# A neighbourhood-attention and Fourier layer: first matmuls on ones, keys in equal pieces, a later split of the u tiles, and another order of the last tile's VectorE work

## The chip, the cores and the metric

The kernel runs on one core of one Trainium2 chip. The metric is the time of one execution in microseconds (us) on the device. It is the median of several runs; the run with a profile is one more execution and has its own time.

## What is computed

The reference is one encoder layer on 256 prompt tokens and, with the same weights, on 2048 sample tokens of width 1024:

```python
h = rms_norm(x, g_pre)
q, k, v, z_a, u_f, z_f = split(h @ w_in)          # six parts, 512 columns each
y_a = neighbourhood_attention(q, k, v, rpb)       # 8 heads of 64, window of 8 x 16 on a grid 64 wide
y_f = fourier_mix(u_f, w_f, b_f)                  # real part of fft2 over tokens and 64-column groups, then @ w_f + b_f
mixed = concat([rms_norm(y_a, g_na) * silu(z_a), rms_norm(y_f, g_f) * silu(z_f)])
x + rms_norm(mixed @ w_out, g_post)
```

All inputs and outputs are float32. A query of the attention sees a slab of 8 grid rows by 32 columns; what lies outside of its own window is masked before the softmax.

## The kernel before, in words

**Products.** A float32 operand is split in a high part, rounded to the type `fp32r`, and a low part, the rest. Every large product is three matmuls on these parts (`mm3`, L163 to L166): high by high (L164), high by low (L165), low by high (L166). The cast to the high part is ScalarE's and the subtraction that gives the low part is VectorE's: `x_split` (L283, L284) for the input tiles `xh` and `xl`, `split_w` (L253, L254) for the weights `wc`, L550 and L551 for the later weights `wa`.

**Order.** The order of TensorE's instructions is that of the code from beginning to end. For the other engines it is that of the code in some stretches (the one with the u tiles and the one of the last output tiles among them) and left to a scheduler elsewhere. Each engine runs its own list in order and waits for what its next instruction needs. SyncE (SP) issues the loads and stores, in the same way.

**Stages.** First the v and u projections of the first input tiles, whose operands must first be loaded and split; the row scales of the norm are spread over partitions by matmuls with a 128x128 tile of ones (`onesq`, filled on GpSimd at L226, used at L309). Then the remaining projections for the sample tokens, in 16 steps `i`, each of seven products `j` of 12 matmuls. Into the steps 9 to 14 the u tiles are woven. Then the Fourier mixing, the attention together with the output product of earlier tiles, and at the end the 18 output tiles of 128 tokens.

**u tiles.** There are 16 of them. A tile is loaded (`u_load`, L364 to L368), split (`u_split`: cast to the high part on ScalarE at L371, low part on VectorE at L372) and multiplied with the first Fourier matrix (`u_stage1`: three matmuls into `pz`, a copy, a store to `ZD`). L915 says when: the tile whose load stands ahead of product x is split three products later and multiplied five products later. In the same products VectorE and ScalarE split the next weights (`wa`, L550 and L551), VectorE does the sums after a product (`u` at L931, `f` at L854), and the bias tables of the attention are prepared: at one product of a step the VectorE subtraction of `t_mask` (L585, tile `mt`), then its three GpSimd additions (L589).

**Attention.** Four head pairs by nine groups of 256 queries: the prompt, and row blocks R0 to R3 in two halves each. A group has two column blocks `b` with `n` keys each: 160 and 160 for the prompt; 264 and 352 (or 352 and 264) in R0; 360 and 480 in R1 and R2; 288 and 384 in R3. The keys are cut in pieces of 128 and a rest (`prep_v`, L1126 to L1131): the pieces of `v` are loaded with the key on the partition, by one DMA for the full pieces and one for the rest. `transp` (L1454) turns the probabilities `w` into `pt` piece by piece on TensorE (L1460) and copies them out of PSUM, one head on ScalarE (L1462) and one on VectorE; `pv` (L1468) multiplies piece by piece (L1476), the key being the contracted dimension, so that a matmul uses as many rows of the array as its piece has keys.

**End.** The last output tile (`last_tile`, L1666) has its second half in two products of 384 and 128 columns (L1673). After each, `evac` (L1627 on VectorE, L1630 on ScalarE) scales it, adds, and sums squares. `residual(b, n)` (L1661) finishes the two halves of the tile before it.

Of the kernel before, what the change touches and what calls it, by code (L numbers as in the profile page):

```python
# [10 lines left out]
F32 = mybir.dt.float32  # L11
# [157 lines left out]
def build(tc, A, O):  # L169
    nc = tc.nc  # L170
# [42 lines left out]
    ps = es.enter_context(tc.tile_pool(name="ps", bufs=3, space=PSUM))  # L213
# [7 lines left out]
    onesq = hp.tile([128, 128], F32, name="onesq")  # L221
    csm = hp.tile([128, 80], F32, name="csm")
    rmask = hp.tile([128, 48], F32, name="rmask")
    nc.gpsimd.memset(onesq, 1.0)

    def gt(shape, dtype, name):  # L226
        return gp.tile(shape, dtype, tag="g", name=name)
# [401 lines left out]
    for kp in range(4):  # L629
        ks = slice(2 * kp, 2 * kp + 2)  # L630
        v = part(RV[kp // 2], kp)
# [107 lines left out]
    for b in range(16):  # L739
# [11 lines left out]
        if b < 8:  # L751
            x, y = divmod(b, 2)
# [7 lines left out]
        p = mmt(512)[:, :TP]  # L760
# [3 lines left out]
        o = st.tile([128, 256], F32, tag="f", name="f", bufs=3)  # L764
        if kind % 2:
            i, d = p, o
        else:
            i = p.rearrange("p (b r c) -> p b r c", b=2, c=32)
            d = o.rearrange("p (r b c) -> p b r c", b=2, c=32)
# [46 lines left out]
    for i in range(16):  # L816
# [15 lines left out]
        o = [st.tile([128, 1024], F32, tag="f", name="f", bufs=3) for x in range(2)]  # L832
# [32 lines left out]
        for j in range(7):  # L865
            if i in (0, 8):
                if j in (0, 3):
                    w_load(i + 1 + j // 3)
                if i == 0 and j == 0:
                    a_split(0, 6)  # L870
                if i == 0 and j == 1:
                    row_scales(10, 8)
                if i == 0 and j == 2:
                    diag_group(1)
                if i == 0 and j == 4:
                    spread_group(1)
                if j == 2:
                    w_sums(i + 1)
                for x in {3: (0, 1), 4: (2, 3), 5: (4, 5), 6: (6,)}.get(j, ()):
                    a_split(i + 1, x)  # L880
            elif i not in (7, 15):
                if j == 0:
                    w_sums(i + 1)
                a_split(i + 1, j)
                if j == 3 and i < 14 and i != 6:
                    w_load(i + 2)
            elif i == 7:
                if j in (3, 4):
                    op_load(j - 3)
                if j in (5, 6):  # L890
                    op_split(j - 5)
                if j == 5:
                    wo_load(0)
            if sg == 0:
                x, y = divmod(7 * (pr - 1) + j, 14)
                if x in (0, 1):
                    if y == 0:
                        n_load(x)
                    elif 3 <= y < 7:
                        n_scale(x, *divmod(y - 3, 2))  # L900
                    elif 7 <= y < 12:
                        n_diff(x, y - 7)
                if pr == 6 and j in (2, 5):
                    (b_split if j > 2 else b_get)(0)
                if pr == 7 and j:
                    b_get(j)
                    if j > 2:
                        b_split(j - 2)
            if i == 2 and j == 0:
                for t, n in ((gmix, "gmix"), (bfs, "bf"), (dnyq, "dnyq"), (rmask, "rmask"), (csm, "csmask")):  # L910
                    nc.sync.dma_start(t, A[n])
                nc.sync.dma_start(cm, A["cmask"].rearrange("p (b x) -> p b x", b=2))
            if i == 5 or 8 <= i < 15:
                t_step(max(0, i - 7), j)
            for f, d in ((u_load, 0), (u_split, 3), (u_stage1, 5)):  # L915
                x = 7 * pr + j - 7 - d
                if sg and 0 <= x < 36 and x % 7 in (0, 2, 4):
                    f(x // 7 * 3 + x % 7 // 2)
            if i == 15 and j in (1, 3, 4, 5):
                if j == 1:  # L920
                    d2 = [load_d(0), load_d(1)]
                else:
                    zgs.append(load_z(j - 3))
            if 9 <= i < 15 and j == 2:
                v_copy(i - 9)
            p = mmt(512)
            aw = aop[i, j]
            bh, bl = bnew[sg, j]
            for k in range(4):
                mm3(nc, p, aw[:, 0, k], aw[:, 1, k], bh[:, k], bl[:, k], k == 0, k == 3)  # L930
            add = lambda o, u: nc.vector.tensor_tensor(out=e_(o), in0=uu[u], in1=p, op=ALU.add)  # L931
            if j == 0:
                nc.scalar.copy(e_("u0"), p)
            elif j == 1:
                comb(0, 0, "u0", p)
            elif j == 2:
                add("u2", "u0")
            elif j == 3:
                add("u4", "u2")
            elif j == 4:  # L940
                comb(1, 1, "u4", p)
                add("u3", "u2")
            elif j == 5:
                comb(1, 0, "u3", p, ALU.subtract)
                store(1)
            else:
                comb(0, 1, "u4", p)
                store(0)
# [165 lines left out]
    def prep_v(g):  # L1114
        cs = slice(g["pr"] * 128, g["pr"] * 128 + 128)
        g["v"] = jl.tile([128, 7, 128], F32, tag="v", name="v", bufs=VB)
        g["ch"], j = [], 0
        for b, (c0, w) in enumerate(g["t"]):
            n = g["nr"] * w
            if g["R"] is None:  # L1120
                src = vP[b]
            else:
                src = vD[2 * g["hc"] + b][K0[g["R"]]:K0[g["R"]] + g["nr"]]
            src = src.rearrange("r c e -> (r c) e")
            f = n // 128
            nc.sync.dma_start(g["v"][:, j:j + f], src[:128 * f, cs].rearrange("(j p) e -> p j e", p=128))  # L1126
            if n % 128:
                nc.sync.dma_start(g["v"][:n % 128, j + f], src[128 * f:, cs])
            ch = [(128 * x, min(128, n - 128 * x), j + x) for x in range((n + 127) // 128)]
            g["ch"].append(ch)  # L1130
            j += len(ch)  # L1131
        g["za"] = jl.tile([128, 256], F32, tag="za", name="za", bufs=VB)
        nc.sync.dma_start(g["za"], zD[1, cs, g["ts"]])
# [84 lines left out]
    for t, (g, x) in enumerate(zip(G, (0, 640))):  # L1218
        g["w"] = []
        for c0, w in g["t"]:  # L1220
            n = 2 * g["nr"] * w
# [126 lines left out]
    V = nc.vector  # L1348
# [104 lines left out]

    def transp(g, b):  # L1454
        ch = g["ch"][b]
        n = len(ch) * 128
        o = jp.tile([128, 2, 512], F32, tag="pt", name="pt", bufs=PB)
        for h in range(2):
            for j, (c0, nk, v) in enumerate(ch):
                nc.tensor.transpose(ptb[h][:nk, j * 128:j * 128 + 128], g["w"][b][:, h, c0:c0 + nk], ident)  # L1460
            if h == 0:
                nc.scalar.copy(o[:, h, :n], ptb[h][:, :n])  # L1462
            else:
                V.tensor_copy(o[:, h, :n], ptb[h][:, :n])
        g["pt"] = g.get("pt", []) + [o]

    yt = {}
# [186 lines left out]
    def residual(d, n):  # L1654
        of, xt, s = d["of"], d["xt"], d["r"][:, 0:1]
        ns = slice(n * 512, n * 512 + 512)
        if "og" in d:
            V.scalar_tensor_tensor(out=xt[:, ns], in0=d["og"][:, ns], scalar=s, in1=xt[:, ns], op0=ALU.mult,
                                   op1=ALU.add)
        else:  # L1660
            V.scalar_tensor_tensor(out=of[:, ns], in0=ptb[n], scalar=s, in1=of[:, ns], op0=ALU.mult, op1=ALU.mult)  # L1661
            nc.gpsimd.tensor_tensor(out=xt[:, ns], in0=of[:, ns], in1=xt[:, ns], op=ALU.add)
        nc.sync.dma_start(O["yo"][d["t"] * 128:d["t"] * 128 + 128, ns], xt[:, ns])


    def last_tile(d, b):  # L1666
        og = d["og"] = gt([128, D], F32, "og")
        nc.gpsimd.tensor_tensor(out=og[:, :512], in0=d["of"][:, :512], in1=gpb[:, :512], op=ALU.mult)
        for q, ns in enumerate((slice(512, 896), slice(896, 1024))):
            p = ps.tile([128, 384], F32, tag="a", name="pl", bufs=3)[:, :ns.stop - ns.start]  # L1670
            for j in range(12):
                c, x = divmod(j, 3)
                nc.tensor.matmul(p, (d["l"] if x == 2 else d["h"])[:, c], WO[x == 1][:, c, ns], start=j == 0,  # L1673
                                 stop=j == 11)
            if q == 0:
                factor(b)
                residual(b, 0)
            evac(d, p, ns, 1 + 2 * q)
        residual(b, 1)
        sa = d["sa"]  # L1680
        V.tensor_scalar(sa[:, 0:1], sa[:, 0:1], sa[:, 1:2], None, ALU.add)
        part_sum(sa)
        guess(d, 3)
        V.tensor_tensor(out=og[:, 512:], in0=ptb[1], in1=d["of"][:, 512:], op=ALU.mult)
        factor(d, 3)
        for n in range(2):
            residual(d, n)
# [49 lines left out]
```

## Time and profile before

| | before |
|---|---|
| time, median of 3 runs | 988.64 us (988.61 to 988.85) |
| time of the profiled execution | 989.52 us |
| its span | 987.4 us |
| TensorE (PE) busy | 970.9 us, 98% |
| VectorE (DVE) busy | 703.6 us, 71% |
| ScalarE (ACT) busy | 501.7 us, 51% |
| GpSimd (POOL) busy | 428.3 us, 43% |
| main DMA queue (q1) | 277.62 MB, 79.9% of 16 engines' span |

The span runs from the first to the last instruction; 2.1 us of the profiled execution's time lie around it. PEld is TensorE loading its stationary operand, which overlaps the matmuls. A row of the timeline gives the start in us, the duration in us, the engine, the line, the operation with its output and inputs, the shape, how many instructions are put together in the row (x3), and in brackets how long the engine stood idle just before and what it waited for. A matmul's duration includes the time in which it passes through the array, so that successive matmuls overlap: their cost is the distance between starts. In the shape of a matmul such as 96*64 96x128 the first number is the contracted dimension, the rows of the array it uses.

### The profile page before, as it was taken

The page shows a single profiled execution, that of the slowest core. Times are in us where ns is not written, and L with a number is a line of the kernel's source. Part 1 is how long each engine was busy: PE and PEld are TensorE (multiplying, and loading weights), DVE is VectorE, ACT ScalarE, POOL GpSimd, SP SyncE. Part 2 cuts the span into 40 slices and gives each one's busy share as a digit, 9 for nine tenths or more (in the row PEclk, how much of TensorE's full clock was granted, in tenths as well). Part 3 has the DMA queues.
Part 4 walks back from the last instruction along what each step waited for, and adds up shares of the span by engine and source line. Part 5 has one row for each costly group of instructions (what it writes and reads, how often), then busy time and mean ns, then how long its engine had stood idle before and what let it go on. Part 6 is the DMA issues. An engine that isn't in the chain of part 4 may idle for free.

```text
span 987.4 us, 17038 instructions
## 1 busy us (share of the span) xinstructions
PE 970.9 (98%) x5774; PEld 805.5 (82%) x5774; DVE 703.6 (71%) x1301; ACT 501.7 (51%) x1083; POOL 428.3 (43%) x400
## 2 busy tenths in 40 slices
PE   7999999999999999999999999999999999999997
PEld 6889988888888878878887879778787887888886
DVE  6378987777866777777976446775665665659997
ACT  6836676433224533333344255677666675644443
POOL 3100002464741102755755033566587686534444
PEclk9999999999999999999999999999999999999999
DMA  9899686566839997598989887697768799779993
GB/s 327 303 380 340 190 330 249 173 221 247 308 148 358 347 387 260 218 337 313 322 314 339 294 312 296 218 277 263 247 213 260 261 309 315 224 245 340 344 338 125
DMA packets 147046, 278.70 MB, mean 282 GB/s; under 512 B 14160, under 2 KB 85136, under 8 KB 143568
## 3 DMA queue, kind: packets, MB, share of 16 engines
q1 hardware_dynamic: 146960, 277.62, 79.9%
q8 instruction: 46, 0.75, 0.3%
q14 instruction: 40, 0.33, 0.1%
HBM read 183.19 MB, written 101.71 MB: 289 GB/s over the span
## 4 chain that ended last, share of the span: by engine, by line
PE 48%; DMA 2%; DVE 1%; issue 1%; ACT 0%; POOL 0%; SPq 0%; DVEq 0%; ACTq 0%; POOLq 0%
PE po L1406 19%; PE pv L1476 6%; PE ptb L1460 5%; PE s L1155 4%; PE mm L165 2%; PE mm L164 2%; PE mm L166 2%; PE pab L1000 2%; DMA ut<-uN 1%; PE py L164 1%; PE py L166 1%; PE py L165 1%; DMA tb<-tD 1%; DVE ut L372 0%; PE ppq L1038 0%
## 5 line engine op out<-in xcount | busy, mean ns | idle before, releaser
L164 PE MATMUL mm<-xh,wa 128*128 128x512 f32 x448 | 174.4, 389 | 0.0
L165 PE MATMUL mm<-xl,wa 128*128 128x512 f32 x448 | 174.3, 389 | 0.0
L166 PE MATMUL mm<-xh,wa 128*128 128x512 f32 x448 | 174.3, 389 | 0.0
L536 POOL TENSOR_TENSOR ws<-wr 128x512 f32<-128x512 f32 x16 | 22.5, 1408 | 238.8 <-DMA wr<-wz 223.5
L1189 POOL TENSOR_SCALAR w<-w,m 128x480 f32<-128x480 f32 (+6 forms) x136 | 83.3, 625 | 64.6 <-DVE m L1186 50.6
L165 PEld LDWEIGHTS mm<-xl,wa 128*128 128x128 f32 x448 | 84.1, 188 | 17.5
L166 PEld LDWEIGHTS mm<-xh,wa 128*128 128x128 f32 x448 | 84.1, 188 | 17.5
L164 PEld LDWEIGHTS mm<-xh,wa 128*128 128x128 f32 x448 | 84.1, 188 | 17.5
L1406 PE MATMUL po<-wo,yh 128*128 128x512 f32 x272 | 90.4, 413 | 0.0
L1182 ACT ACTIVATE w<-w,m 128x480 f32<-128x480 f32 (+6 forms) x136 | 79.2, 585 | 15.5 <-DVE m L1177 15.5
L1406 PE MATMUL po<-w,yh 128*128 128x512 f32 x280 | 86.7, 391 | 0.0
L551 DVE TENSOR_TENSOR wa<-wr,wa 128x512 fp32r<-128x512 f32 x60 | 62.3, 1045 | 32.0 <-ACT wa L550 31.9
L1177 DVE CUSTOM_DVE_ANT_1 w<-s,tb 128x360 f32<-128x360 f32 (+5 forms) x124 | 62.5, 541 | 9.1 <-PE s L1155 8.5
L165 PE MATMUL mm<-vl,xh 128*128 128x512 f32 x168 | 65.6, 390 | 0.9 <-DVE vl L482 0.9
L589 POOL TENSOR_TENSOR mt<-mt,rmask 128x880 f32<-128x880 f32 (+2 forms) x24 | 53.7, 2250 | 27.6 <-DMA ut<-uN 15.5
L166 PE MATMUL mm<-vh,xl 128*128 128x512 f32 x168 | 65.4, 389 | 0.0
L164 PE MATMUL mm<-vh,xh 128*128 128x512 f32 x168 | 65.4, 389 | 0.0
L1476 PEld LDWEIGHTS pv<-pt,v 128*64 128x64 f32 (+4 forms) x896 | 47.4, 135 | 19.0 <-issue 14.9
L1476 PE MATMUL pv<-pt,v 128*64 128x128 f32 (+4 forms) x896 | 62.3, 280 | 0.0
L854 DVE TENSOR_TENSOR f<-u,mm 128x512 f32<-128x512 f32 x64 | 43.6, 681 | 25.2 <-PE mm L166 15.4
L1406 PEld LDWEIGHTS po<-w,yh 128*128 128x128 f32 x280 | 52.3, 188 | 10.9 <-issue 0.2
L1460 PE MATMUL ptb<-ident,w 128*128 128x128 f32 (+4 forms) x428 | 59.9, 277 | 0.0
(253 smaller groups left out, 2384.9 us busy)
## 6 DMA issues: line engine op xcount, KB each, us to landing
wr<-wz SPq DMA_DIRECT2D x48, 512.0 KB
vl<-sD SPq DMA_DIRECT2D x20, 512.0 KB
xm<-xm SPq DMA_DIRECT2D x9, 1024.0 KB
oD<-ofs SPq DMA_DIRECT2D x18, 512.0 KB
of<-oD SPq DMA_DIRECT2D x18, 512.0 KB
yr<-yD SPq DMA_DIRECT2D x34, 256.0 KB
zD<-f SPq DMA_DIRECT2D x16, 512.0 KB
woD<-wo SPq DMA_DIRECT2D x16, 512.0 KB
```

The source lines that it names most:

```text
L164: nc.tensor.matmul(out, lh, rh, start=first, stop=False)
L165: nc.tensor.matmul(out, lh, rl, start=False, stop=False)
L166: nc.tensor.matmul(out, ll, rh, start=False, stop=last)
L551: nc.vector.tensor_tensor(out=o[:, 1], in0=src, in1=o[:, 0].bitcast(F32), op=ALU.subtract)
L589: nc.gpsimd.tensor_tensor(out=o, in0=i, in1=rmask[:, m0:m0 + n].unsqueeze(2).to_broadcast([128, n, 80]), op=ALU.add)
L854: nc.vector.tensor_tensor(out=dst(f, b), in0=src(uu[u]), in1=src(p), op=op)
L1177: nc.vector.tensor_tensor_reduce(out=rows(g["w"][b][:, h, :n], w), in0=rows(g["s"][2 * b + h][:, :n], w), in1=tv, scale=1.0, scalar=3.0e38 ...
L1182: nc.scalar.activation(w, w, AF.Exp, bias=m[:, h:h + 1], scale=-1.0, accum_out=m[:, 2 + h:3 + h])
L1189: nc.gpsimd.tensor_scalar(w, w, m[:, 4 + h:5 + h], 1.0, ALU.mult, ALU.mult)
L1406: nc.tensor.matmul(p, (d["l"] if x == 2 else d["h"])[:, c], w(n, int(x == 1), c), start=j == 0, stop=j == 11)
L1460: nc.tensor.transpose(ptb[h][:nk, j * 128:j * 128 + 128], g["w"][b][:, h, c0:c0 + nk], ident)
L1476: nc.tensor.matmul(p[hs, b], g["v"][:nk, v, hs], g["pt"][b][:nk, h, j * 128:j * 128 + 128], start=j == 0, stop=j == len(ch) - 1)
```

## The change

1. After the memset of `onesq`, ten float32 matmuls of ones by ones, 128x128 each, go to a PSUM tile of their own (`idle`), which nothing reads. They are the first instructions of TensorE.
2. The n keys of a column block are cut in as few pieces as before, but of equal size (rounded up): 160 in 80 and 80; 264 in three of 88; 352 in 118, 118 and 116; 360 in three of 120; 480 in four of 120; 288 in three of 96; 384 in three of 128, as before. Only 352 leaves a last piece that differs, and only there the `v` load still has a second DMA. The copies out of the transposes take the partitions of a piece alone.
3. A u tile is split four products after its load and multiplied six products after it.
4. In the last tile `residual(b, 1)` stands ahead of the second `evac` instead of behind it.

```diff
     nc.gpsimd.memset(onesq, 1.0)
 
+    idle = ps.tile([128, 512], F32, tag="c", name="idle", bufs=1)
+    for x in range(10):
+        nc.tensor.matmul(idle[:, :128], onesq, onesq, start=True, stop=True)
...
-            for f, d in ((u_load, 0), (u_split, 3), (u_stage1, 5)):
+            for f, d in ((u_load, 0), (u_split, 4), (u_stage1, 6)):
                 x = 7 * pr + j - 7 - d
                 if sg and 0 <= x < 36 and x % 7 in (0, 2, 4):
                     f(x // 7 * 3 + x % 7 // 2)
...
-            f = n // 128
-            nc.sync.dma_start(g["v"][:, j:j + f], src[:128 * f, cs].rearrange("(j p) e -> p j e", p=128))
-            if n % 128:
-                nc.sync.dma_start(g["v"][:n % 128, j + f], src[128 * f:, cs])
-            ch = [(128 * x, min(128, n - 128 * x), j + x) for x in range((n + 127) // 128)]
+            m = -(-n // 128)
+            z = -(-n // m)
+            f = n // z
+            nc.sync.dma_start(g["v"][:z, j:j + f], src[:z * f, cs].rearrange("(j p) e -> p j e", p=z))
+            if n % z:
+                nc.sync.dma_start(g["v"][:n % z, j + f], src[z * f:, cs])
+            ch = [(z * x, min(z, n - z * x), j + x) for x in range(m)]
...
-        n = len(ch) * 128
+        n, z = len(ch) * 128, ch[0][1]
...
-                nc.scalar.copy(o[:, h, :n], ptb[h][:, :n])
+                nc.scalar.copy(o[:z, h, :n], ptb[h][:z, :n])
...
-                V.tensor_copy(o[:, h, :n], ptb[h][:, :n])
+                V.tensor_copy(o[:z, h, :n], ptb[h][:z, :n])
...
             if q == 0:
                 factor(b)
-                residual(b, 0)
+            residual(b, q)
             evac(d, p, ns, 1 + 2 * q)
-        residual(b, 1)
```

**What moves on TensorE at the start.** The first instructions of TensorE, before and then changed; `mm` is the first projection, `wc` a split weight, `xh` and `xl` the split input.

```order
L1732 UNCONDITIONAL_BRANCH
L164 MATMUL mm<-wc,xh 128x512
L165 MATMUL mm<-wc,xh 128x512
L166 MATMUL mm<-wc,xl 128x512
L164 MATMUL mm<-wc,xh 128x512
```

```order
L1737 UNCONDITIONAL_BRANCH
L228 MATMUL idle<-onesq 128x128 x10
L164 MATMUL mm<-wc,xh 128x512
L165 MATMUL mm<-wc,xh 128x512
L166 MATMUL mm<-wc,xl 128x512
```

The projection is the same and starts behind ten matmuls that need nothing but the memset of `onesq`.

**What moves on VectorE among the u tiles.** One place in step 10, before and then changed: `wa` is a split weight (L551, L555 after), `mt` the subtraction of `t_mask` (L585, L589 after), `ut` the low part of a u tile (L372, L376 after), `u` and `f` are sums after a product (L931 and L854, L935 and L858 after).

```order
L585 TENSOR_TENSOR mt<-csm,mt 128x1200
L372 TENSOR_TENSOR ut<-ut 128x512
L931 TENSOR_TENSOR u_3887<-u_3861,mm 128x512
L551 TENSOR_TENSOR wa<-wr,wa 128x512
L854 TENSOR_TENSOR f<-u_3887,mm 128x16x32
L931 TENSOR_TENSOR u_3912<-u_3861,mm 128x512
L551 TENSOR_TENSOR wa<-wr,wa 128x512
L372 TENSOR_TENSOR ut<-ut 128x512
L854 TENSOR_TENSOR f<-u_3912,mm 128x16x32
```

```order
L589 TENSOR_TENSOR mt<-csm,mt 128x1200
L935 TENSOR_TENSOR u_3896<-u_3865,mm 128x512
L555 TENSOR_TENSOR wa<-wr,wa 128x512
L376 TENSOR_TENSOR ut<-ut 128x512
L858 TENSOR_TENSOR f<-u_3896,mm 128x16x32
L935 TENSOR_TENSOR u_3923<-u_3865,mm 128x512
L555 TENSOR_TENSOR wa<-wr,wa 128x512
L858 TENSOR_TENSOR f<-u_3923,mm 128x16x32
L555 TENSOR_TENSOR wa<-wr,wa 128x512
```

The first `ut` has gone from right behind `mt` to two places later, behind a sum and a weight split; the second has gone past a sum and a weight split too, and now stands just below the piece shown.

**What moves on TensorE in the attention.** The transposes of one R0 group (L1460, L1466 after): `w` holds the probabilities, the first number of the shape is the keys of a piece; between them stand matmuls of the output product (L1406, L1412 after). This group has 352 keys and then 264, before and then changed:

```order
L1460 MATMUL ptb<-ident,w 128x128 x2
L1460 MATMUL ptb<-ident,w 96x128
L1460 MATMUL ptb<-ident,w 128x128 x2
L1460 MATMUL ptb<-ident,w 96x128
L1406 MATMUL po<-wo_5193,yh 128x512 x2
L1406 MATMUL po<-wo_5193,yl 128x512
L1406 MATMUL po<-wo_5194,yh 128x512 x2
L1406 MATMUL po<-wo_5194,yl 128x512
L1460 MATMUL ptb<-ident,w 128x128 x2
L1460 MATMUL ptb<-ident,w 8x128
L1460 MATMUL ptb<-ident,w 128x128 x2
L1460 MATMUL ptb<-ident,w 8x128
```

```order
L1466 MATMUL ptb<-ident,w 118x128 x2
L1466 MATMUL ptb<-ident,w 116x128
L1466 MATMUL ptb<-ident,w 118x128 x2
L1466 MATMUL ptb<-ident,w 116x128
L1412 MATMUL po<-wo_5201,yh 128x512 x2
L1412 MATMUL po<-wo_5201,yl 128x512
L1412 MATMUL po<-wo_5202,yh 128x512 x2
L1412 MATMUL po<-wo_5202,yl 128x512
L1466 MATMUL ptb<-ident,w 88x128 x6
```

The number of transposes and their places are the same; pieces of 8, 32 and 96 keys beside pieces of 128 have become pieces of nearly one size. The matmuls of `pv` follow the same pieces.

## The prediction

> **What bounds the kernel.** I read the page's first part, then the list of waits of TensorE, then the timelines of the places that the list names, and last the chain of waits for the attention. The engines' busy times:
>
> ```profile
> PE 970.9 (98%) x5774; PEld 805.5 (82%) x5774; DVE 703.6 (71%) x1301; ACT 501.7 (51%) x1083; POOL 428.3 (43%) x400
> ```
>
> TensorE is busy all the time but for 16.5 us of the span of 987.4. The two longest entries in its list of waits (sum, times, longest):
>
> ```profile
> PE mm L164 <- ACT xh L283: 5.4, 1, 5.4
> PE pz L165 <- DVE ut L372: 1.5, 2, 0.9
> ```
>
> So a change gains in two ways: it removes a wait of TensorE, and both of these are touched here, or it makes TensorE's own instructions shorter or fewer. What other engines save is worth nothing unless TensorE waits for it. The first wait is for the first operands; behind it the matmuls start like this:
>
> ```profile
> 5.39 0.80 PE L164 MATMUL mm<-wc,xh 128*128 128x512 f32 x1 [5.39 <-ACT xh L283]
> ...
> 10.79 0.63 PE L164 MATMUL mm<-wc,xh 128*128 128x512 f32 x1
> 11.22 0.52 PE L165 MATMUL mm<-wc,xh 128*128 128x512 f32 x1
> 11.57 0.40 PE L166 MATMUL mm<-wc,xl 128*128 128x512 f32 x1
> 11.80 0.39 PE L164 MATMUL mm<-wc,xh 128*128 128x512 f32 x1
> ...
> 12.49 0.39 PE L164 MATMUL mm<-wc,xh 128*128 128x512 f32 x1
> ```
>
> The columns are start, duration, engine and line. Until 11.22 one start follows the other by 0.43 us, from 11.57 on by 0.23: TensorE runs at half its speed for its first six microseconds of work. (The page's clock row rounds this away; the spacing shows it.)
>
> **Part 1, ones first.** The ones are there before a microsecond is over, and the price of such a matmul stands where the row scales are spread, eight float32 matmuls of the same shape, each of two instructions:
>
> ```profile
> 0.73 0.20 POOL L224 MEMSET onesq<- 128x128 f32 x1 [0.29 <-POOLq L1728]
> 52.37 1.95 PE L309 MATMUL iv<-dg,onesq 128*128 128x128 f32 x16
> 54.08 0.48 PE L164 MATMUL mm<-wc,xh 128*128 128x512 f32 x1
> ```
>
> Sixteen instructions in 1.71 us, 0.107 each. Ten matmuls are 20 of them: 2.1 us at full speed, 4.3 at half, from 0.93+0.1 to 5.3. The operands come at 5.39, so they delay nothing, and they cover nearly all of the wait. If about six microseconds of work must go by before the speed doubles, four of them are now spent ahead of the first product, and it doubles some two microseconds into it.
>
> The 14 matmuls that start from 5.39 to 11.22 cost 0.20 too much each, 2.8 us in all. I don't take all of that, since at full speed the operands set the pace:
>
> ```profile
> 11.24 0.75 DVE L284 TENSOR_TENSOR xl<-xr,xh 128x256 fp32r<-128x256 f32 x2
> ```
>
> The two low parts end at 11.99, and the products that need them start at 12.49 at the earliest before. With the splits queued as they are, and each pacing three matmuls, I place the product that starts at 12.49 near 10.5, that is 1.95 us earlier. The ends: 0.9, if the speed doubles only at about 9; 2.3, if it has doubled by 5.4 and the splits keep up. Behind this place TensorE never waits again up to the spread, so the gain is kept; the weights of the u products, the next thing that could be late, must then be there 2 us sooner, and their splits wait for loads and not for TensorE. I take 1.95. [...]
>
> **Part 2, equal pieces.** The chain of waits gives the `pv` blocks as a whole (start, duration, number of instructions):
>
> ```profile
> 624.37 1.47 PE pv L1476 x16
> ...
> 631.13 1.76 PE pv L1476 x24
> ...
> 638.45 1.61 PE pv L1476 x24
> ...
> 646.46 1.69 PE pv L1476 x28
> ```
>
> These are the prompt's group (pieces of 128, 32, 128, 32 keys), the two halves of R0 (128, 128, 8, 128, 128, 96, and then 128, 128, 96, 128, 128, 8), and a half of R1 (128, 128, 104, then three of 128 and one of 96). The two R0 blocks have the same instructions, yet the one that changes from 8 keys back to 128 within costs 0.15 more. I read it so: each step between a piece of 128 (or 96, or 104) and a piece of 32 or 8 costs 0.15 us, and a step between 128 and 96 or 104 costs nothing. The check: three steps in the prompt's block leave 1.47-0.45 = 1.02 for 16 instructions; the line from there to 1.69 for 28 gives 1.47 for 24; with one step 1.62, with two 1.77. The rows say 1.61 and 1.76. The R3 halves go by the same steps (128, 128, 32), and theirs are
>
> ```profile
> 677.92 1.76 PE pv L1476 x24
> ...
> 684.75 1.61 PE pv L1476 x24
> ```
>
> After the change no block has a small piece. The steps that go, for each head pair: 3 in the prompt's block, 2+1 in R0, 2+1 in R3, so 9; four pairs, 36 steps of 0.15: 5.4 us. Rounding in the rows makes 5.3 as likely, and I take 5.3. The bounds: pieces of 80 or 88 keys were never seen. They lie between 32 and 96; if 88 next to 118 costs a step as 32 does, the eight R0 blocks give back 8 x 0.15 = 1.2, leaving 4.1. From above, 36 x 0.155 = 5.6. I take them to be like 96, the nearest row.
>
> The number of matmuls is the same. The transposes contract over 128 queries whatever the piece, and their time does not depend on its size:
>
> ```profile
> L1460 PE MATMUL ptb<-ident,w 128*128 128x128 f32 x308 | 53.4, 279 | 0.0
> ...
> L1460 PE MATMUL ptb<-ident,w 128*32 128x128 f32 x28 | 7.3, 272 | 0.0
> ```
>
> The copies out of PSUM keep their columns and lose partitions; I take them as long as before, and TensorE's list has no wait of over 0.2 us for them. At nothing. The `v` loads are 56 fewer issues on SP. How long one has to land:
>
> ```profile
> 688.16 0.37 SPq L1126 DMA_DIRECT2D v<-vD  x1
> ```
>
> ```profile
> 698.93 1.83 PE L1476 MATMUL pv<-pt,v 128*64 128x128 f32 x24
> ```
>
> The block that uses this load, the last large one of its group, starts 10.8 us after the issue. [...]
>
> **Part 3, u tiles.** Three tiles came late:
>
> ```profile
> 426.03 0.39 PE L164 MATMUL pz<-ut,f1h 128*128 128x512 f32 x1
> 427.32 0.50 PE L165 MATMUL pz<-ut,f1h 128*128 128x512 f32 x1 [0.91 <-DVE ut L372]
> ...
> 475.55 0.39 PE L164 MATMUL pz<-ut,f1h 128*128 128x512 f32 x1
> 476.06 0.50 PE L165 MATMUL pz<-ut,f1h 128*128 128x512 f32 x1
> ...
> 524.27 0.39 PE L164 MATMUL pz<-ut,f1h 128*128 128x512 f32 x1
> 525.21 0.50 PE L165 MATMUL pz<-ut,f1h 128*128 128x512 f32 x1 [0.56 <-DVE ut L372]
> ```
>
> The second matmul should start 0.23 after the first. It starts 1.06, 0.28 and 0.71 too late, and is 0.11 longer each time: 2.4 us in all. One product more between load and split, and as much between load and use, removes all three. But the split also moves against VectorE's and GpSimd's other work, and that is where part of it comes back:
>
> ```profile
> 509.31 0.68 DVE L372 TENSOR_TENSOR ut<-ut 128x512 fp32r<-128x512 f32 x1
> 514.20 2.68 DVE L372 TENSOR_TENSOR ut<-ut 128x512 fp32r<-128x512 f32 x1
> ```
>
> ```profile
> 509.48 6.86 POOL L589 TENSOR_TENSOR mt<-mt,rmask 128x880 f32<-128x880 f32 x3 [4.23 <-DVE mt L585]
> ```
>
> The same split takes 0.68 where GpSimd stands still and 2.68 where it falls within the three mask additions (509.48 to 516.34): it ends at 516.88, 0.54 behind the last addition, as if it had to let the running addition finish first. Six of the 16 tiles (the first, and every third from it) were split just ahead of these additions; now they are split one product later, in their midst. Worked for step 13: the additions take 880, 960 and 1200 columns, so the second ends near 509.48 + 6.86 x 1840/3040 = 513.6, and the split, which then comes behind a weight split that the first addition held up, ends near 514.2. Its use was at 512.03 and moves by a product of 12 matmuls and what is between, 2.9 us, to 514.9: 0.7 to spare, enough. But the additions don't begin at the same place in each step:
>
> ```profile
> 467.03 1.41 DVE L585 TENSOR_TENSOR mt<-csm,mt 128x1200 f32<-128x1200 f32 x1 [0.48 <-DMA ut<-uN]
> ...
> 508.00 1.40 DVE L585 TENSOR_TENSOR mt<-csm,mt 128x1200 f32<-128x1200 f32 x1
> ```
>
> ```profile
> 469.43 0.39 PE L164 MATMUL pz<-ut,f1h 128*128 128x512 f32 x1
> ...
> 512.03 0.39 PE L164 MATMUL pz<-ut,f1h 128*128 128x512 f32 x1
> ```
>
> In step 13 the subtraction ahead of the additions starts 4.0 us before the use, in step 11, where VectorE waited for a load, 2.4 us before it: 1.6 later. In step 9 it had waited too (the first stall above). There the split comes 1.6-0.7 = 0.9 late if the whole shift reaches it, and 0.2 if little over half of it does, since VectorE has some idle time between the products; I take the middle, 0.55, for each: two stalls, 1.1 us. So 2.4-1.1 = 1.3 us gained. The ends: 2.4 gained if none comes late; above, the second rival. `z`'s copy and store move one product later as well, behind the table stores on SP, and nothing on TensorE waits for them. The three buffers of `ut` are held one product longer, six instead of five; three tiles are loaded in seven products, so a buffer is still free a product before its next load.
>
> **Part 4, the last tile.** VectorE's second evacuation waits for TensorE:
>
> ```profile
> 980.15 0.35 DVE L1627 SCALAR_TENSOR_TENSOR of<-pl,inva,of 128x128 f32<-128x128 f32 x1 [0.53 <-PE pl L1673]
> 980.41 0.74 DVE L1661 SCALAR_TENSOR_TENSOR of<-ptb,sr,of 128x512 f32<-128x512 f32 x1
> 981.07 0.20 DVE L1681 TENSOR_SCALAR sa<-sa 128x1 f32<-128x1 f32 x1
> ```
>
> The residual (0.74, some 0.57 of it before the next can start) now fills these 0.53 us ahead of it, so the evacuation starts 0.03 later. The sum at 981.07 waited for the residual before; now it waits for ScalarE's square of what was evacuated, at the same time within 0.04. At nothing; between 0.3 gained, if the store that leaves earlier counts, and 0.1 lost.
>
> **The sum.** 1.95 + 5.3 + 1.3 + 0 = 8.55. The profiled execution of 989.52 (its span and 2.1 around it) comes to 981.0; it lies 0.9 above the median of the runs, 988.64, so the median comes to 980.1. 0.2% of it, about 2 us, is what a measurement here can tell from no change.
>
> **Rivals.**
> 1. *The speed doubles late.* The ten matmuls are a little short of the wait or keep too small a part of TensorE busy, and the gain is 0.9 or nothing. For it: the moment of doubling was seen once. Against: the same kind of matmul ran at full pace at 52.37. Time: 980.1 + 1.05 to 1.95, so 981.2 to 982.1.
> 2. *More u tiles wait for GpSimd.* If four or five of the six tiles wait for an addition and not two, each 0.55 to 1.0 late, the stalls are 2.4 to 4.5 instead of 1.1: 981.4 to 983.5.
> [...]
> 4. *Equal pieces do nothing.* The 0.15 belongs to something else than the step, such as the wait for the last `v` piece: 985.4. Against: it repeats to 0.01 in the R0 and R3 blocks above.
>
> **Chances.** Forecast (with the u stalls between none and three) 0.64; speed late 0.14; more u stalls 0.10; part of the gain lost by rival 3, or rival 4: 0.07; nearly all of it lost by rival 3: 0.03; slower by over 0.2% by rival 3: 0.02. The first four are faster by over 0.2%: 0.95; the fifth is within it: 0.03; slower 0.02. Range: below, all u stalls gone (1.1), the clock at its upper end (0.35) and 5.6 for the pieces add to 978.4, so 978.2; above, rivals 1 and 2 nearly whole, 982.8.
>
> **What would show it.** In the profile after: matmuls on ones from about 1.0 to 5.3, and the product of 12.49 near 10.5. [...] In the list of waits, `pz` for `ut` twice, 0.5 each; more than four times is rival 2. The end from 980.15 on as before but for the order. Wrong altogether would be a time over 984, or blocks of 24 that still differ by 0.15.

## The result

The changed kernel takes 981.71 us (median of 4 runs, 980.97 to 984.02) against 988.75 for the kernel before; the ratio is 0.9932 (95% interval 0.9915 to 0.9949). Run once more beside the experiments it took 981.0 (980.32 to 982.47), 0.9923 (0.9909 to 0.9937). The forecast was 980.1 with a range of 978.2 to 982.8.

The profiled execution of the changed kernel is its slowest, 984.02 with a span of 982.2; the others had spans of 979.2 to 980.0. So its trace shows one thing, the late u tiles, at its worst; the second profile (span 979.2) shows it milder. Of the changed kernel's page, the engines:

```profile
PE 968.8 (99%) x5794; PEld 808.7 (82%) x5794; DVE 704.9 (72%) x1301; ACT 501.7 (51%) x1083; POOL 425.6 (43%) x400
```

TensorE is busy for nearly all of the span, with 13.4 us of it idle instead of 16.5. Its list of waits, same kernel and profile (sum, times, longest):

```profile
PE pz L165 <- DVE ut L376: 2.8, 5, 1.0
PE idle L228 <- POOL onesq L224: 1.0, 1, 1.0
PE s L1161 <- POOL ql L1144: 0.7, 1, 0.7
PE mm L166 <- DVE wl L574: 0.6, 3, 0.2
PE mm L165 <- DVE wc L258: 0.5, 2, 0.3
```

The wait of 5.4 for the first operands is gone; there are two new ones of 0.2 to 0.3 for the weight splits behind it (`wc`). The wait for u tiles has not gone but grown, from two times to five. And the wait of the scores for `ql`, the low part of q, went from 0.2 to 0.7. The start, in the timeline of TensorE:

```profile
0.99 4.50 PE L228 MATMUL idle<-onesq 128*128 128x128 f32 x20 [0.99 <-POOL onesq L224]
5.25 0.48 PE L164 MATMUL mm<-wc,xh 128*128 128x512 f32 x1
5.71 0.51 PE L165 MATMUL mm<-wc,xh 128*128 128x512 f32 x1
...
7.05 0.50 PE L165 MATMUL mm<-wc,xh 128*128 128x512 f32 x1 [0.28 <-DVE wc L258]
...
10.57 0.50 PE L164 MATMUL mm<-wc,xh 128*128 128x512 f32 x1
...
23.45 0.39 PE L164 MATMUL mm<-wc,xh 128*128 128x512 f32 x1
```

The row at 10.57 is the 19th product matmul, which started at 12.49 before: 1.92 earlier. The row at 23.45 is the 73rd, 24.73 before: 1.28 earlier. The `pv` blocks, from the chain of waits: a prompt's, one of R1, the two of R3 and the first of R0 in the next head pair:

```profile
624.23 1.05 PE pv L1482 x16
653.66 1.68 PE pv L1482 x28
...
676.81 1.46 PE pv L1482 x24
683.34 1.46 PE pv L1482 x24
...
696.98 1.46 PE pv L1482 x24
```

In the kernel before they were 1.47, 1.69, 1.76, 1.61 and 1.76. All 36 blocks together, from the start of each to the start of what follows, take 54.38 us instead of 59.77.

### The profile page after: what moved, and what is told of

Its sections match the earlier page's. It is cut to its first block, busy times and chain, and to the rows that moved or that the text cites. A ratio compares the mean times of both kernels' runs of the same rounds, so it can differ in the third digit from the quotient of the medians.

```text
span 982.2 us, 17009 instructions
## 1 busy us (share of the span) xinstructions
PE 968.8 (99%) x5794; PEld 808.7 (82%) x5794; DVE 704.9 (72%) x1301; ACT 501.7 (51%) x1083; POOL 425.6 (43%) x400
## 4 chain that ended last, share of the span: by engine, by line
PE 45%; DMA 6%; DVE 3%; issue 1%; ACT 1%; POOL 1%; SPq 1%; DVEq 0%; POOLq 0%; ACTq 0%
PE po L1412 18%; PE ptb L1466 5%; PE pv L1482 5%; PE s L1161 4%; PE mm L165 2%; PE mm L166 2%; PE mm L164 2%; PE pab L1004 2%; DMA ut<-uN 1%; DMA wr<-wz 1%; PE py L164 1%; PE py L166 1%; PE py L165 1%; DVE ut L376 1%; DMA qD<-f 1%
## 5 line engine op out<-in xcount | busy, mean ns | idle before, releaser
L1195 POOL TENSOR_SCALAR w<-w,m 128x480 f32<-128x480 f32 (+6 forms) x136 | 80.6, 606 | 61.6 <-DVE m L1192 49.7
L1412 PE MATMUL po<-wo,yh 128*128 128x512 f32 x272 | 90.5, 414 | 0.0
L555 DVE TENSOR_TENSOR wa<-wr,wa 128x512 fp32r<-128x512 f32 x60 | 66.3, 1114 | 28.7 <-ACT wa L554 28.7
L1412 PE MATMUL po<-w,yh 128*128 128x512 f32 x280 | 86.6, 391 | 0.0
L593 POOL TENSOR_TENSOR mt<-mt,rmask 128x880 f32<-128x880 f32 (+2 forms) x24 | 51.6, 2164 | 33.2 <-DMA ut<-uN 15.2
L858 DVE TENSOR_TENSOR f<-u,mm 128x512 f32<-128x512 f32 x64 | 43.5, 680 | 27.4 <-PE mm L166 24.9
L1412 PEld LDWEIGHTS po<-w,yh 128*128 128x128 f32 x280 | 52.3, 188 | 10.9 <-issue 0.2
L1466 PE MATMUL ptb<-ident,w 128*120 128x128 f32 (+5 forms) x428 | 59.7, 277 | 0.0
L1482 PEld LDWEIGHTS pv<-pt,v 120*64 120x64 f32 (+6 forms) x896 | 48.2, 136 | 12.9 <-issue 10.0
L1470 DVE COPY pt<-ptb 120x384 f32<-120x384 f32 (+6 forms) x72 | 41.0, 569 | 24.1 <-PE ptb L1466 23.4
```

What stands on the lines that cost most here:

```text
L555: nc.vector.tensor_tensor(out=o[:, 1], in0=src, in1=o[:, 0].bitcast(F32), op=ALU.subtract)
L593: nc.gpsimd.tensor_tensor(out=o, in0=i, in1=rmask[:, m0:m0 + n].unsqueeze(2).to_broadcast([128, n, 80]), op=ALU.add)
L858: nc.vector.tensor_tensor(out=dst(f, b), in0=src(uu[u]), in1=src(p), op=op)
L1195: nc.gpsimd.tensor_scalar(w, w, m[:, 4 + h:5 + h], 1.0, ALU.mult, ALU.mult)
L1412: nc.tensor.matmul(p, (d["l"] if x == 2 else d["h"])[:, c], w(n, int(x == 1), c), start=j == 0, stop=j == 11)
L1482: nc.tensor.matmul(p[hs, b], g["v"][:nk, v, hs], g["pt"][b][:nk, h, j * 128:j * 128 + 128], start=j == 0, stop=j == len(ch) - 1)
```

## The experiments

Two theories stood at the beginning: the parts add up and each does what its own rows say (A), or the stretch of the u tiles is paced by its loads and takes back what is gained ahead of it (B). The first four kernels each make one part of the change on the kernel before; their edits are the four parts of the diff above, one at a time.

**Ones alone.**

> The kernel before with the ten matmuls on ones alone. Theory A (the parts add up): products run at full speed from about 6.4, the matmul that started at 12.49 starts near 10.6, some 0.6 us of it is lost again to the weight splits within the first 25 us, and 1.3 us remain to the end: ratio 0.9987. Theory B (the stretch of the u tiles, 420 to 540 us, is paced by its loads, so that time gained ahead of it is given back there): the same start, but more wait of VectorE for the mask's load and more of pz for ut, and at most 0.5 us left: ratio 0.9995 or more.

Measured: 988.12, ratio 0.9994 (0.9985 to 1.0003). The 19th matmul starts at 10.40 and the 73rd at 23.13. From there to the first Fourier product of the next stage it is 550.0 us, against 550.7 before, so in these two profiles nothing more is taken back in the stretch of the u tiles, which speaks against B. The ratio doesn't decide: it lies nearer to B's forecast (0.9995) than to A's (0.9987), and its interval holds both, since the start of the kernel before varies (below).

**Pieces alone.**

> The kernel before with the keys in equal pieces alone. Theory A and B: 5.3 us gained, all of it in the 36 steps between large and small pieces (pv blocks of 16 instructions shorter by 0.44, R0 and R3 blocks by 0.29 and 0.14, R1 and R2 the same): ratio 0.9946. [...]

Measured: 984.46, ratio 0.9952 (0.994 to 0.9965). The blocks take 54.38 us, 5.39 less than before, but the stretches between them 199.76 instead of 198.91. No `pv` waits for `v`. The size of the steps is shown; what grew between the blocks comes up again behind the last experiment.

**u tiles alone.**

> The kernel before with the u tiles split and multiplied one product later, alone. Theory A: the split now falls into the GpSimd additions whatever the phase, so that the stalls of pz grow from 2.1 to about 3.5 us: 1 to 1.5 slower, ratio 1.001 to 1.0015. Theory B: the stalls after the change came from TensorE being 1 to 2 us earlier while the mask's loads were not; without that the stalls stay under 1.5 us: 0.5 to 1.3 faster, ratio 0.9987 to 0.9995.

Measured: 987.23, ratio 0.999 (0.9977 to 1.0002). The late starts of `pz`, summed over the tiles (distance of its first three matmuls less 0.23 each), are 1.26 us, against 2.40 before. That is not A's growth; the ratio is within B's forecast, but its interval takes in no change at all.

**Tail alone.**

> The kernel before with the last tile's VectorE order alone. Both theories: no difference beyond 0.3 us (ratio 0.9997 to 1.0003); the second evacuation of the last tile starts 0.03 us later, the sum behind it at the same time within 0.05.

Measured: 987.8, ratio 0.999 (0.9981 to 0.9998). Both theories missed. VectorE's end in this kernel:

```profile
978.07 0.61 DVE L1627 SCALAR_TENSOR_TENSOR of<-pl,inva,of 128x384 f32<-128x384 f32 x1
978.59 0.74 DVE L1661 SCALAR_TENSOR_TENSOR of<-ptb,sr,of 128x512 f32<-128x512 f32 x1
979.25 0.34 DVE L1627 SCALAR_TENSOR_TENSOR of<-pl,inva,of 128x128 f32<-128x128 f32 x1
979.51 0.21 DVE L1680 TENSOR_SCALAR sa<-sa 128x1 f32<-128x1 f32 x1
```

```profile
979.68 0.31 ACT L1630 ACTIVATE jk<-of 128x128 f32<-128x128 f32 x1 [0.30 <-DVE of L1627]
```

The sum `sa` now starts 0.26 behind the second evacuation, and before ScalarE has begun to square what that gave. Before, it started 0.92 behind it, with the residual of 0.74 between. So it adds the first two sums of squares alone, the later of which ScalarE had finished at 979.39, and doesn't wait for the third, which enters later. From TensorE's last matmul to the end it is 6.67 us instead of 7.29: 0.62 gained, all of it on VectorE.

The next three kernels start from the changed one, and the changed kernel ran beside them.

**The changed kernel again.**

> The changed kernel once more, beside the next three. Theory A (a split in the midst of the GpSimd additions is late whatever happens elsewhere): pz waits for ut in five or six tiles again, 3 us or more in the sum of starts. Theory B (late only when the mask's load is late against the products, which differs from run to run): the sum comes out clearly otherwise than the 3.6 us of the first profile, 1 to 2.5. Both: products at full speed from 5.1 to 5.3 us on, the same within 0.2 as in the first profile, since the ones start at a fixed place.

Measured: 981.0 (0.9923, 0.9909 to 0.9937). The late starts of `pz` are 1.93 us in two tiles, where the first profile had 4.16 in five: the stalls differ from run to run, as B had it, and they make 2.2 of the 3.0 us between the two profiles.

**Without the u part.**

```diff
-            for f, d in ((u_load, 0), (u_split, 4), (u_stage1, 6)):
+            for f, d in ((u_load, 0), (u_split, 3), (u_stage1, 5)):
```

> The changed kernel with the old places of the u tiles (split after three products, use after five), so with ones, pieces and tail alone. Theory A: no split in the midst of the additions, pz late in three tiles, 2.1 us as before; 1 to 1.5 us faster than the changed kernel: 0.9985 to 0.999 of it. Theory B: 2 to 2.5 us of stalls, since TensorE comes earlier and the loads don't; 0 to 1 us slower than the changed kernel.

Measured: 983.17, ratio 0.9941 (0.9928 to 0.9953), that is 2.2 us more than the changed kernel beside it and 1.5 more than its first measurement, while the two profiled executions differ by 0.7, as their late starts do (2.65 and 1.93 us). So the u part seems to gain, though in its first profile it seemed to lose; how much is open, since the intervals of the two ratios overlap.

**Split early, use late.**

```diff
-            for f, d in ((u_load, 0), (u_split, 4), (u_stage1, 6)):
+            for f, d in ((u_load, 0), (u_split, 3), (u_stage1, 6)):
```

> The changed kernel, but the u tile is split after three products as before and used after six as in the change: the split stays right behind the mask's subtraction and ahead of the GpSimd additions, with a product more until its use. Both theories: no wait of pz for ut of over 0.3 us in any tile, so 1 to 3.5 us less than the changed kernel's profile, and a time of 978.5 to 980.5, ratio to the kernel before 0.990 to 0.992. If the stalls stay, the split does not wait for the additions but for its load.

Measured: 979.22 (978.91 to 979.8), ratio 0.9903 (0.9889 to 0.9916), no late start at all. The same tile in the changed kernel's first profile and here; first VectorE, GpSimd and TensorE of the changed kernel:

```profile
444.29 1.41 DVE L589 TENSOR_TENSOR mt<-csm,mt 128x1200 f32<-128x1200 f32 x1 [1.52 <-DMA mt<-tr]
445.61 0.68 DVE L935 TENSOR_TENSOR u<-u,mm 128x512 f32<-128x512 f32 x1
446.21 1.77 DVE L555 TENSOR_TENSOR wa<-wr,wa 128x512 fp32r<-128x512 f32 x1
447.91 2.28 DVE L376 TENSOR_TENSOR ut<-ut 128x512 fp32r<-128x512 f32 x1
```

```profile
445.77 6.47 POOL L593 TENSOR_TENSOR mt<-mt,rmask 128x880 f32<-128x880 f32 x3 [5.73 <-DVE mt L589]
```

```profile
448.88 0.39 PE L164 MATMUL pz<-ut,f1h 128*128 128x512 f32 x1
450.24 0.50 PE L165 MATMUL pz<-ut,f1h 128*128 128x512 f32 x1 [0.97 <-DVE ut L376]
```

And with the early split:

```profile
443.41 1.41 DVE L589 TENSOR_TENSOR mt<-csm,mt 128x1200 f32<-128x1200 f32 x1 [1.71 <-DMA mt<-tr]
444.79 0.69 DVE L376 TENSOR_TENSOR ut<-ut 128x512 fp32r<-128x512 f32 x1
```

```profile
444.89 6.92 POOL L593 TENSOR_TENSOR mt<-mt,rmask 128x880 f32<-128x880 f32 x3 [5.34 <-DMA ut<-uN]
```

```profile
447.94 0.39 PE L164 MATMUL pz<-ut,f1h 128*128 128x512 f32 x1
448.17 0.39 PE L165 MATMUL pz<-ut,f1h 128*128 128x512 f32 x1
```

In both the subtraction `mt` waits 1.5 to 1.7 us for the mask's load. With the early split `ut` takes 0.69 right behind it and ends 2.5 us ahead of its use. In the change it comes behind `wa`, both within the additions, and they take 1.77 and 2.28; it ends 1.3 behind the start of its use. The `u` sum between `mt` and `wa`, which has one input in PSUM, takes its usual 0.68. So of these three the two with both inputs in SBUF are the slow ones; how the additions hold them up is not shown.

**Mask one product later.** The changed kernel with `t_mask` at products 4 to 6 instead of 3 to 5; the mask's load stays where it was and has a product more to land:

```diff
-        if j == 0:
-            t_load(x)
-        for q in {3: (0, 1), 4: (2,), 5: (3,)}.get(j, ()):
+        for q in {4: (0, 1), 5: (2,), 6: (3,)}.get(j, ()):
             t_mask(x, q)
-        if j > 4:
-            t_store(x, j - 5)
+        if j == 6:
+            t_store(x, 0)
...
+            if j == 0 and mt:
+                t_store(max(0, i - 8), 1)
             if i == 5 or 8 <= i < 15:
+                if j == 0:
+                    t_load(max(0, i - 7))
                 t_step(max(0, i - 7), j)
```

> The changed kernel with the subtraction and the three additions of the mask one product later too (and the store of the last table at the head of the next step), so that split and additions stand to each other as in the kernel before, the mask's load has a product more to land, and the use of the u tile is as late as in the change. Theory A and B: the splits of every third tile take 0.68 again, VectorE no longer waits for the mask's load, no wait of pz for ut of over 0.3 us: ratio to the kernel before 0.990 to 0.992. If VectorE still waits for the mask's load, SP issues it later too, and nothing is gained against the changed kernel.

Measured: 979.65, ratio 0.9908 (0.9895 to 0.9922); late starts of 0.08 us in all, and no wait of VectorE for the mask's load. Here the splits that fell in the midst of the additions stand just ahead of them again, with two products until their use. So both remove the stalls: a product more between split and use, or the old order with a product more for the mask's load.

**Mask's load earlier.** What is left is whether the load alone makes the split late.

```diff
-        if j == 0:
+        if j == 0 and not mt:
             t_load(x)
...
             t_store(x, j - 5)
+        if j == 6 and 0 < x < 7:
+            t_load(x + 1)
```

> The changed kernel, but from the second u step on the mask's load is issued by SP at the end of the step before, ahead of two stores that wait for other engines. The split stays within the GpSimd additions. Theory as in the prediction (a split within the additions is in time by 0.7 us when the subtraction starts on time, and late only when the mask's load holds the subtraction up): VectorE waits less than 1 us in all for the mask's load, pz waits for ut in at most one tile, sum of its late starts under 1 us; 1 us faster than the changed kernel, ratio to the kernel before 0.9905 to 0.9915. Rival (the additions alone are enough to make the split late): the stalls stay at 2 to 4 us in two to five tiles, ratio 0.992 to 0.993.

Measured: 985.1, ratio 0.9967 (0.9955 to 0.998). VectorE no longer waits for the load among the u tiles, yet two tiles are late by 1.78 and 1.32, and the late starts are 3.84 us in all. (1.0 us more is a wait for a weight split at 97.8, far from the edit.) This is 4.1 us more than the changed kernel's 981.0, beyond what the rival forecast too; of the 3.4 us between the two profiles the late starts and that wait make 2.9, and the rest is open. The theory that only the load makes the split late falls. VectorE here, at the same tile:

```profile
442.64 0.69 DVE L860 TENSOR_TENSOR f<-u,mm 128x512 f32<-128x512 f32 x1 [4.03 <-DMA ZD<-z]
...
445.05 1.40 DVE L589 TENSOR_TENSOR mt<-csm,mt 128x1200 f32<-128x1200 f32 x1
...
446.96 1.77 DVE L555 TENSOR_TENSOR wa<-wr,wa 128x512 fp32r<-128x512 f32 x1
448.66 2.28 DVE L376 TENSOR_TENSOR ut<-ut 128x512 fp32r<-128x512 f32 x1
```

A sum `f` waited 4.0 us for a buffer that a store of `z` still held, and that store now stands behind the mask's load on SP. So `mt` starts later than before (445.05, not 444.29 or 443.59), without waiting for its own load. My reading is that the split is late when any DMA holds VectorE up ahead of `mt`, and that it then pays the additions on top; the load is only one such DMA.

**Four ones.**

```diff
-    for x in range(10):
+    for x in range(4):
         nc.tensor.matmul(idle[:, :128], onesq, onesq, start=True, stop=True)
```

> The changed kernel with four matmuls on ones instead of ten: 8 instructions, from 1.0 to about 2.7 us, then TensorE is idle until its operands come at 5.25. [...]

Measured: 982.09, ratio 0.9932 (0.992 to 0.9944). TensorE's start:

```profile
0.99 2.08 PE L228 MATMUL idle<-onesq 128*128 128x128 f32 x8 [0.99 <-POOL onesq L224]
5.24 0.80 PE L164 MATMUL mm<-wc,xh 128*128 128x512 f32 x1 [2.17 <-ACT xh L287]
...
10.65 0.48 PE L164 MATMUL mm<-wc,xh 128*128 128x512 f32 x1
10.97 0.39 PE L165 MATMUL mm<-wc,xh 128*128 128x512 f32 x1
11.20 0.39 PE L166 MATMUL mm<-wc,xl 128*128 128x512 f32 x1
...
12.12 0.39 PE L164 MATMUL mm<-wc,xh 128*128 128x512 f32 x1
```

The speed doubles at 10.8, the 19th matmul starts at 12.12: like a start without ones (8.8 to 13.8 and 11.17 to 14.13 in the four profiles). If the work since the start alone decided, the 2.1 us of ones would count: as an estimate from the 6.1 us between the first product and the doubling in the kernel before, it would then come near 9.2, and it came 1.6 later. But the same distance lies between 3.6 and 8.3 us in the four profiles without ones, so one profile doesn't decide it, and what sets the moment is not shown.

**q split earlier.** On top of "split early, use late":

```diff
         if g:
-            soft(g, 1)
             if k + 1 < len(G):
                 split_q(G[k + 1])
+            soft(g, 1)
```

> The kernel with the late use of the u tiles (split after three products, use after six), and the split of the next group's q set ahead of the last softmax scaling of a group instead of behind it, on ScalarE and GpSimd. Theory (part of the gain of the equal pieces is given back because TensorE now reaches the scores before GpSimd has made the low part of q): no TensorE instruction of the scores waits for ql any more, the stretches between the pv blocks are 0.3 to 0.8 us shorter in sum than with the late use alone (199.2 us), and the time is 0.3 to 0.8 lower: ratio to the kernel before 0.9895 to 0.990. Rival (GpSimd is simply too slow there, and the scaling of w that is now later holds the transposes up): the waits move from the scores to the transposes, and the sum stays at 199.2 or grows.

Measured: 976.99 (976.55 to 977.61), ratio 0.9881 (0.9863 to 0.9899), the fastest of all. The stretches between the `pv` blocks fall from 199.20 to 197.27 us. The list of waits of TensorE's weight loads had, in the kernel before and with the late use alone,

```profile
PEld s L1155 <- POOL ql L1138: 1.8, 4, 0.7
```

```profile
PEld s L1161 <- POOL ql L1144: 2.1, 6, 0.5
```

and this row is gone. The theory's mechanism is right; the gain is 1.9 us instead of 0.3 to 0.8, since it also takes away the wait that the kernel before had. The rival shows in one stretch, where the transposes now wait instead (below).

## Why the prediction was right, point by point

The measured gain is 7.0 us, or 7.5 in the second measurement, of the 8.55 forecast. The time lies within the range because the largest part, the pieces, was sized rightly in its blocks; the ones came out short, the tail over, the u tiles one way or the other, and that these errors partly cancel is luck. The upper end of the range, 982.8, is not "rivals 1 and 2 nearly whole": by the prediction's own figures they are 982.1 and 983.5, each alone.

**Ones: 1.95 forecast, 1.3 found.** The 19th matmul started at 12.49, 11.90, 14.13 and 11.17 in the four profiles of before and of single parts without ones, on average 12.42, and at 10.21 to 10.81, on average 10.5, in the eight with ten ones: 1.9, as forecast; that the one profile on which the forecast rests, 12.49, lay near the mean is luck. The step that failed is "TensorE never waits again up to the spread, so the gain is kept": the 73rd matmul came at 24.67 and 23.35 on average, so 0.6 is lost in between, where the changed kernel waits for weight splits. What I had not foreseen is that the ones take away a spread. Without them the clock opens between 8.8 and 13.8 us from run to run, so a comparison with any one profile gives 0 to 3 us.

**Pieces: 5.3 forecast, 5.39 found in the blocks, about 4.5 to 5.1 to the end.** The price of a step, 0.15, and the count of 36 were right, and pieces of 80, 88, 116, 118 and 120 rows behave like 96: from start to start 1.02 us for 16 instructions, 1.46 to 1.47 for 24 and 1.68 for 28. What the sum left out was the wait for another operand: being earlier, TensorE reaches the scores before GpSimd has split q. A group of the second head pair, the scores before and then in the changed kernel's second profile:

```profile
752.76 0.28 PE L1155 MATMUL s<-kl,qh 64*128 64x264 f32 x2
752.90 0.39 PE L1155 MATMUL s<-kh,ql 64*128 64x264 f32 x2
```

```profile
747.00 0.29 PE L1161 MATMUL s<-kl,qh 64*128 64x264 f32 x2
747.37 0.40 PE L1161 MATMUL s<-kh,ql 64*128 64x264 f32 x2
```

The second row now follows by 0.37 and not 0.14. The last experiment moved the split of q ahead, and these waits went. Stretch by stretch, five of the 35 are longer with the pieces alone by 0.12 to 0.25 us, which is more than the whole 0.85. In four of them the weight loads wait 0.15 to 0.26 longer for `ql`, and with the split ahead they are as short as before, within 0.01, or shorter. In the fifth (5.07 before, 5.27) half goes to the scores and half to the second transposes; with the split ahead the scores' part goes and the transposes wait longer (5.33).

Rival 3 of the chances, that the loads of 118 keys come late, counts on a delay that no run shows: in the nine profiles with equal pieces these loads have landed 5.4 to 8.1 us behind their issue, 1.8 us or more ahead of the block that needs them. The loads of the last piece, of 116, come closer: 1.1 ahead. So no `pv` waits for `v`. A trace records each step of the counter that tells of a load's landing: sixteen for a load of two pieces of 128 keys, three for one of two pieces of 118, the first of them within 0.6 us of the issue. In the trace before there are 14 steps for 104 keys and 9 for 8. What the number of steps has to do with a load's time is not shown.

**u tiles: 1.3 forecast, 0.5 to 2.2 found.** Between the changed kernel and the one without this part there are 1.5 to 2.2 us, and the part alone gave 0.999 (0.9977 to 1.0002). In the profiles the late starts are 1.94 to 3.25 us with the old places (five profiles) and 0.74 to 4.16 with the new (four): on average 2.6 and 2.0, a difference smaller than the spread. The mechanism was right (the split in the midst of the additions, late where the subtraction is late), but the step "two stalls", for the steps 9 and 11, failed: which tiles are late is not a property of two steps, it differs from run to run. The load of the mask as the only cause was wrong, by the early load. The second rival, more late tiles, is what the first profile shows, with five; the second has two.

**Tail: 0 forecast, 0.62 found** alone and 0.3 to 0.5 beside the other parts, by the step "now it waits for ScalarE's square of what was evacuated", which it doesn't: the sum reads two columns of which the later was done 0.12 us before. In all nine kernels with this order VectorE's last instruction ends 3.78 or 3.79 us behind TensorE's last matmul, 4.40 in the four without; with equal pieces what follows VectorE's last instruction takes 0.1 to 0.35 longer, for a reason that is open. In the kernel before, ScalarE's read and the residual ended within 0.15 us of each other, and I took both for dependences; the columns of `sa` in the code would have told.

**The sum** by what was found, with 4.8 for the pieces, 0.4 for the tail and 0.5 to 2.2 for the u tiles, is 1.3 + 4.8 + 0.4 + 0.5 = 7.0 up to 8.7, which takes 988.75 to 981.7 or 980.0; measured 981.7 and 981.0.

## What to carry to other kernels

Where TensorE is the bound, count the steps between contracted sizes (0.15 us each here) and not only the instructions: equal pieces gave five of the seven microseconds for no work less. A gain on the bound engine meets the next operand, so look at once for what was just in time (here the low part of q, for which TensorE's weight loads waited already) and move that too: that was worth 2.2 us more. And where both of its inputs are in SBUF, a short VectorE operation that TensorE waits for belongs ahead of a long GpSimd one, not within it (here 0.69 us right ahead of the mask additions, 2.28 among them).

## What the runs showed of the hardware

- TensorE's speed doubles near the start: in the kernel before, one start follows the other by 0.43 us until 11.22 and by 0.23 from 11.57. The doubling came 3.6 to 5.7 us behind TensorE's first instruction in the eight runs with ten ones (by the trace's record of the granted clock, at 4.63 to 6.69 us, ones from 0.99), 3.6 to 6.1 behind the first product in three runs without, and only 8.3 behind it in the run of the u part alone, where the first three microseconds of products had waits for operands of 0.5 and 0.4 us beyond their pace. With four ones and a pause of 2.2 it doubled at 10.8, no earlier than in starts without ones (8.8 to 13.8). What sets the moment is not shown.
- A step between contracted sizes of 128 rows and 32 or 8 costs 0.15 us; steps between 128 and 96 or 104, and between 88 and 116 or 118, cost nothing that these blocks show (24 instructions take 1.46 to 1.47 us, where one step made 1.61 and two 1.76), and blocks of 80 or 120 rows throughout go at the same pace (1.02 us for 16 instructions; 1.68 for 28, where rows of 128, 104 and 96 took 1.68 to 1.69).
- A VectorE subtraction of 0.68 us with both its inputs in SBUF takes 0.8 to 2.7 us when it starts while a mask addition runs on GpSimd (2.28 for each of the six splits in the changed kernel); a sum with one input in PSUM keeps 0.67 to 0.69.
- A load of 118 partitions, 118 KB, raises its counter in three steps and lands in 5.4 to 8.1 us; one of 128 partitions and 128 KB in the kernel before, sixteen steps and 2.2 to 8.3, 3.7 at the median.
